# The delta rule's chain first in the scheduler, and the second block's convolutions straight from PSUM, in a two-block float32 kernel

## The chip, the cores and the metric

One NeuronCore of a Trainium2 chip runs the whole program. The metric is the time of one execution in microseconds (us), as the device measures it; a single profiled execution gives the trace from which all durations below are read. The engines carry the profile's names: PE is TensorE (matmuls, with its weight loads shown apart as PEld), DVE is VectorE, ACT is ScalarE, POOL is GpSimd, and SP is the engine whose queue issues most of the DMAs.

## The reference

A sequence of 256 tokens of width 1024 passes through two blocks in float32. The first has two layers of feed-forward network, hybrid mixer and feed-forward network. The second, where nearly all of the change lies, mixes tokens in two ways side by side and ends with a mixture of experts (MoE) with 32 experts. Its gated delta rule takes most of what follows:

```
def gated_deltanet(q_in, k_in, v_in, z, a, b, conv_w, a_log, dt_bias, out_norm):
    qkv = causal_conv_silu(jnp.concatenate([q_in, k_in, v_in], axis=-1), conv_w)
    q, k, v = jnp.split(qkv.astype(jnp.float32), 3, axis=-1)
    q = l2_norm(q...) * (HEAD_DIM ** -0.5);  k = l2_norm(k...)
    ...
    m = jnp.where(strict, jnp.einsum('bhncd,bhnsd->bhncs', kb, k) * decay, 0.0)
    t_mat = lax.linalg.triangular_solve(eye + m, eye, left_side=True, lower=True)
    ...
    o = rms_norm(o, out_norm) * jax.nn.silu(zf)

def sliding_window_attention(q, k, v, q_norm, k_norm, sinks, positions):
    q = rope(rms_norm(q, q_norm), positions);  k = rope(rms_norm(k, k_norm), positions)
    ...
```

`causal_conv_silu` is a convolution of four taps along the tokens with a SiLU behind it; `rope` turns pairs of elements by the cosine and sine of position times frequency.

## The kernel before

A float32 matmul is made of three products of rounded parts: weights and activations are each split into a high and a low part (fp32r), and high times high, low times high and high times low are summed in PSUM. ACT makes the high part (L304) and DVE the low part (L305).

In block 2 the input projection is done in pieces, in the order of `BLOCK2`: `q` and `k` (queries, keys and values of the attention), `n` (the gates), `2 3` (the two convolved column groups of the delta rule's keys), `0 1` (its queries), `4 5` (its values), `z` (its output gate). `S`, `G` and `V` start three generators beside them: the attention (`swa`), the delta rule (`gdn`) and its queries and values (`gqv`). A generator issues some instructions and yields; the planner goes round them. Instructions are then placed by a scheduler that fills each engine's queue, and code within `high_priority` goes ahead there by the number in `PRIO`. What a reader sees in a trace is each engine's queue, worked off strictly in its order.

The projection's column groups go through `fm`: for each half of 128 columns, `fm` multiplies the high weights with both activation parts at once (512 wide, L398), and the low weights with the high part (256 wide, L401). The two parts lie in one PSUM tile side by side and have to be added: ACT copies one to SBUF (L179) and DVE adds the other (L181). `conv2` then makes four taps of it, one on ACT (L1339) and three on DVE (L1341), and the SiLU (ACT L1344, DVE L1345). Three PSUM tiles (`pj`) hold the projection's sums, so that a new column group starts when the one three before it has been read. `z_out` reads z's sums on ACT (L1300) and DVE (L1301).

The chain of the delta rule is long. PE sums the squares of the keys (L1388); a reciprocal square root follows (`rsqrt_w`, L321 to L326, on DVE and ACT); sk (L1444) is broadcast by PE (L1453); four products with decays give gMT (L1480). The triangular solve is an explicit inverse: the 32 x 32 diagonal blocks are masked (L1593), transposed, and solved row by row in a loop of 15 steps on DVE (L1612, L1614), spread out as gX and gXt (L1619, L1622, L1625), and then joined to larger blocks by matmuls (from L1654 and L1673). In the attention, rotary angles and norms (L1712 to L1723) come ahead of transposes (L1745), scores (L1760 to L1762) and products (L1780, L1790). The end of the block is the output projection, 512 wide (L342 to L345), into which the two halves of the delta rule's output enter through gzo (L1537, L1541).

Of the kernel before, what the change touches and what calls it, by code (L numbers as in the profile page):

```python
# [7 lines left out]
F32 = mybir.dt.float32  # L8
# [3 lines left out]
AF = mybir.ActivationFunctionType  # L12
ALU = mybir.AluOpType
# [6 lines left out]
KD = 8  # L20
# [5 lines left out]
EPS2 = 1e-6  # L26
# [2 lines left out]
         'c1 x3 x4 x2 z2 z3 MB g0:0 g2:0 JS g2:3 g2:2 g2:1 g0:2 w2 g0:3 g1:0 JD g0:1 g1:2 w0 g1:3 g1:1 JM w1')  # L29
BLOCK2 = 'q n 2 3 S V G 0 k 4 1 z 5'  # L30

PRIO = {'narrow': 300, 'rope2': 300}

SPARE, SPARE2 = (1, 2), (1,)

# [71 lines left out]
class Net:  # L107
# [272 lines left out]

    def fm(self, xT, w, c0, fn):
        st = {}

        def tile(j):
            def run(wh, wl):
                xh, xl = xT()
                if j == 0:
                    st["a"] = (wh, wl)  # L390
                    return
                mm = self.nc.tensor.matmul
                for q in range(2):
                    ps = self.pj.tile([128, 512], F32, name="ps", tag="ps")
                    c = slice(q * 128, q * 128 + 128)
                    for k in range(KD):
                        h = (st["a"] if k < 4 else (wh, wl))[0]
                        mm(ps.rearrange("p (a b) -> p a b", a=2), h[:, k % 4, c], xh.both(k), start=k == 0, stop=False)  # L398
                    for k in range(KD):
                        l = (st["a"] if k < 4 else (wh, wl))[1]  # L400
                        mm(ps[:, 0:256], l[:, k % 4, c], xh[:, k, :], start=False, stop=k == KD - 1)  # L401
                    fn(q, ps[:, 0:256], ps[:, 256:512])
            return run

        for j in range(2):
            self.W(w[:, 4 * j:4 * j + 4, c0:c0 + 256], 4, 256, tile(j))
# [744 lines left out]
        nc.vector.tensor_scalar(v, v, -1.0, None, op0=ALU.mult)  # L1151


    def rope2(self, tabs):
        nc, I = self.nc, self.I
        P = self.sc([128, 2], I32, "pos")
        nc.sync.dma_start(P, I["positions_2"].rearrange("o (t p) -> p (o t)", p=128))
        for _ in range(5):
            yield
        pf = self.sc([128, 2], F32, "posf")  # L1160
        nc.vector.tensor_copy(pf, P)
        r = self.sc([128, 2, 2, 32], F32, "ang")
        c, s = r[:, 0, :, :], r[:, 1, :, :]
        for tb in range(NB):
            nc.vector.tensor_scalar(c[:, tb, :], self.inv2, pf[:, tb:tb + 1], None, op0=ALU.mult)
        n = self.sc([128, 2, 32], F32, "nrot")
        ts, stt = nc.vector.tensor_scalar, nc.vector.scalar_tensor_tensor
        for m in (4096.0, 1.0):
            ts(n, c, 1.0 / (TWO_PI * m), None, op0=ALU.mult)
            ts(n, n, ROUND, None, op0=ALU.add)  # L1170
            ts(n, n, -ROUND, None, op0=ALU.add)
            for q in PI_PARTS:
                stt(c, n, -q * m, c, op0=ALU.mult, op1=ALU.add)
        ts(c, c, 3.1415925, -3.1415925, op0=ALU.min, op1=ALU.max)
        nc.scalar.activation(s, c, AF.Sin)
        nc.scalar.activation(c, c, AF.Abs)
        ts(c, c, -1.0, math.pi / 2, op0=ALU.mult, op1=ALU.add)
        nc.scalar.activation(c, c, AF.Sin)
        self.rot = {}
        for g in ("q_norm_2", "k_norm_2"):  # L1180
            T = tabs[:, len(self.rot), :, :, :]
            gv = self.v2[g].rearrange("p (a b) -> p a b", a=2)
            for tb in range(NB):
                for i, x in enumerate((c, s)):
                    nc.vector.tensor_tensor(T[:, tb, i, :].rearrange("p (a b) -> p a b", a=2), gv,
                                            x[:, tb:tb + 1, :].to_broadcast([128, 2, 32]), op=ALU.mult)
            self.rot[g] = T


    def modulation(self, ss):  # L1190
# [72 lines left out]
    def block2(self, S_, us):  # L1263
        nc, I = self.nc, self.I
        w = I["w_in_2"][0].rearrange("(k p) n -> p k n", p=128)
        xT = lambda: S_["xT"]
        B = {"done": set(), "pj": False}
        self.B = B

        def alloc():  # L1270
            B["QVc"], B["KB"] = (self.t8([128, 8, S], F32, n) for n in ("gqv", "gkk"))
            t = self.big.tile([128, 2048], F32, name="sqkv", tag="b8")
            B["QV"] = t[:, 0:1536].rearrange("p (t n) -> p t n", t=2)
            self.active.append((self.rope2(t[:, 1536:2048].rearrange("p (g t i d) -> p g t i d", g=2, t=2, i=2)), 1, "rope2"))
            B["zO"] = self.t8([128, 4, 512], F32, "gzo")
        self.DO(alloc)


        def merged(i):
            if ("m", i) not in B:  # L1280
                t = self.t8([128, 8, S], F32R, "merged")
                B["m", i] = (t[:, 0:4, :], t[:, 4:8, :])
            return B["m", i]
        B["merged"] = merged

        def q_out(*ps):
            for tb in range(NB):
                nc.scalar.copy(B["QV"][:, tb, 0:512].rearrange("p (j a d) -> p a j d", a=2, j=4),
                               ps[tb].rearrange("p (a j d) -> p a j d", a=2, j=4))
            B["done"].add("q")  # L1290

        def kv_out(*ps):
            for tb in range(NB):
                nc.scalar.copy(B["QV"][:, tb, 512:768], ps[tb])
            B["done"].add("kv")

        def z_out(*ps):
            for tb in range(NB):
                z = B["zO"][:, tb, :]
                nc.scalar.activation(z, ps[tb], AF.Tanh, scale=0.5)  # L1300
                nc.vector.scalar_tensor_tensor(z, z, 1.0, ps[tb], op0=ALU.add, op1=ALU.mult)  # L1301
            B["done"].add("z")

        B["prefetch"] = lambda: us[0]["gu"]()
        first = True
        for it in BLOCK2.split():
            if it == "q":
                self.tok(xT, w, 2064, q_out, lead=first, spare=SPARE2)
            elif it == "n":
                self.narrow(xT, w, 2048, lambda pd: self.gates(B, pd))  # L1310
            elif it == "k":
                self.tok(xT, w, 2576, kv_out, n=256, lead=first)
            elif it == "z":
                self.tok(xT, w, 1536, z_out, lead=first)
            elif it == "G":
                self.GO(lambda: self.gdn(B), "gdn")
            elif it == "S":
                self.GO(lambda: self.swa(B), "swa")
            elif it == "V":
                self.GO(lambda: self.gdn_qv(B), "gqv")  # L1320
            else:
                j = int(it)
                self.fm(xT, w, j * 256, self.joined(lambda ps, j=j: self.conv2(B, j, ps)))
            first = False
        self.JOIN("swa")
        self.DO(lambda: (B.update(pj=True), B["head"]()))
        wo = I["w_out_2"][0].rearrange("(k p) n -> p k n", p=128)
        pre, fn, B["head"] = self.gated(S_, B)
        self.outp(lambda k: [a[:, k % 4, :] for a in B["m", k // 4]], wo, KD, fn, pre=pre, order=(4, 5, 6, 7, 0, 1, 2, 3),
                  join={4: "gdn"}, pre_at=4, tail=lambda: us[1]["gu"]())  # L1330
# [93 lines left out]
    def gdn(self, B):  # L1424
        nc = self.nc
        heads = lambda a: a.rearrange("p (h d) -> p h d", h=8)
        wide = lambda a, n=8: a.rearrange("p (h o) -> p h o", o=1).to_broadcast([128, n, 64])
# [7 lines left out]
        g, nG, eG = B["g"], B["nG"], B["eG"]  # L1435
        flat = lambda a: a.rearrange("p t h -> p (t h)")

        ps = self.squares(B, kT)
        rk = self.ln_p.tile([128, 3, 8], F32, name="rk", tag="rk")
        lk = self.ln_p.tile([128, 2, 8], F32, name="lk", tag="lk")  # L1440
        sk = self.ln_p.tile([128, 2, 8], F32, name="sk", tag="sk")
        self.rsqrt_w(flat(rk[:, 0:2, :]), flat(ps), 1.0, 4.0 * EPS2)
        yield
        nc.vector.tensor_tensor(sk, rk[:, 0:2, :], B["beta"], op=ALU.mult)  # L1444
        nc.vector.tensor_tensor(rk[:, 2, :], rk[:, 0, :], eG[:, 1, :], op=ALU.mult)
        nc.scalar.activation(lk, rk[:, 0:2, :], AF.Ln)
        nc.vector.tensor_tensor(nG, nG, lk, op=ALU.add)
        for tb in range(NB):
            t = slice(tb * 128, tb * 128 + 128)
            pb = bank([128, 4, 128])  # L1450
# [12 lines left out]
        MT = self.t8([128, 16, 128], F32, "gMT")  # L1463
# [115 lines left out]
    def inverse(self, B, MT, Xt):  # L1579
# [10 lines left out]
        A = self.sc([128, 512], F32, "sub")  # L1590
        for g in range(4):
            p = slice(32 * g, 32 * g + 32)
            tt(A[p, :].rearrange("p (i x m) -> p i x m", i=16, x=2), MT[p, :, p].rearrange("p m (x i) -> p i x m", x=2),  # L1593
               half[p, :].rearrange("p (o x u) -> p o x u", o=1, u=1).to_broadcast([32, 16, 2, 16]), op=ALU.mult)
        yield
        E = self.sc([128, 512], F32, "sub")
        nc.vector.transpose(E, A)
# [721 lines left out]
    def early(self, L):  # L2319
        for _ in range(6):  # L2320
            yield
        self.setup1()
        yield
        yield from self.setup2()
        yield from self.columns(0, L[0])

    def network(self, S_, out):
# [63 lines left out]
```

## Time and profile before

| | us |
|---|---|
| three runs | 2116.33, 2114.21, 2116.43 (median 2116.33) |
| the profiled execution | 2114.26 |
| span of its instructions | 2112.5 |
| mean granted clock of PE | 0.989 of full speed |

The profiled execution is 2.07 us under the median of the runs. Start times below count from the span's start; block 2's projection begins at about 1,640 us and its output projection ends at 1,818 us.

### The profile page before, as it was taken

The numbers are of one execution on the slowest core, as the hardware profiler recorded it, in microseconds if no ns is written. First come the engines' busy times: TensorE is split into PE (matmuls) and PEld (weight loads), VectorE is DVE, ScalarE is ACT, GpSimd is POOL, SyncE is SP. The second block draws the span as 40 slices with busy tenths as digits, with TensorE's granted clock in tenths as the row PEclk, the third lists the DMA queues.
The fourth block names the chain that finished last, engine by engine and source line by source line (L and its number), as shares of the span: only waits on it lengthen the run. The fifth ranks groups of instructions, "written<-read, shape, count | busy, mean of one in ns | idle before, by whom it ended". The sixth has DMA issues, their size and how long they took to land.

```text
span 2112.5 us, 30668 instructions
## 1 busy us (share of the span) xinstructions
PE 2053.8 (97%) x11411; PEld 1642.9 (78%) x11411; DVE 1477.7 (70%) x2785; ACT 1098.8 (52%) x2021; POOL 79.9 (4%) x65
## 2 busy tenths in 40 slices
PE   8999999999999999999999999999998989799998
PEld 7887877888888888888877888888887878545553
DVE  6876688987888667785688896877756885733332
ACT  6554565777655544553565776755543744211211
POOL 0000000100000000000000110000000200101000
PEclk9999999999999999999999999999999979999999
DMA  8875544454668676876544365575674323799895
GB/s 254 293 250 173 174 130 124 140 162 130 201 199 299 198 241 205 272 240 200 160 131 141 106 179 153 162 229 156 185 238 145 103 83 126 264 382 354 339 399 197
DMA packets 278825, 428.64 MB, mean 203 GB/s; under 512 B 21550, under 2 KB 206096, under 8 KB 277648
## 3 DMA queue, kind: packets, MB, share of 16 engines
q1 hardware_dynamic: 278240, 423.48, 61.7%
q0 software_dynamic: 432, 3.15, 0.4%
q8 instruction: 92, 1.51, 0.3%
q14 instruction: 61, 0.50, 0.1%
HBM read 425.50 MB, written 1.07 MB: 202 GB/s over the span
## 4 chain that ended last, share of the span: by engine, by line
PE 86%; DVE 9%; ACT 2%; issue 1%; POOL 1%; DMA 1%; SPq 0%; ACTq 0%; POOLq 0%; DVEq 0%
PE ps L398 27%; PE ps L401 14%; PE ps L2067 6%; PE y L342 5%; PE y L343 5%; PE y L345 4%; PE ps L2109 3%; PE ps L342 3%; PE ps L345 3%; PE ps L343 3%; DVE lo L305 2%; PE y L2122 2%; PE ps L2214 1%; PE y L331 1%; DVE cv L947 1%
## 5 line engine op out<-in xcount | busy, mean ns | idle before, releaser
L305 DVE TENSOR_TENSOR lo<-raw,hi 128x1024 fp32r<-128x1024 f32 (+1 forms) x556 | 659.0, 1194 | 250.1 <-ACT hi L304 172.7
L304 ACT CAST hi<-raw 128x1024 fp32r<-128x1024 f32 (+1 forms) x556 | 556.3, 1028 | 329.0 <-PE y L345 169.3
L398 PE MATMUL ps<-xhl,hi 128*128 128x512 f32 x2336 | 595.9, 396 | 5.2 <-DVE gzo L1301 4.4
L398 PEld LDWEIGHTS ps<-xhl,hi 128*128 128x128 f32 x2336 | 420.3, 189 | 84.0 <-DVE gzo L1301 4.6
L401 PEld LDWEIGHTS ps<-xhl,lo 128*128 128x128 f32 x2336 | 319.3, 190 | 23.0
L401 PE MATMUL ps<-xhl,lo 128*128 128x256 f32 x2336 | 328.6, 283 | 0.0
L342 PE MATMUL y<-hi,hh 128*128 128x512 f32 x352 | 137.3, 390 | 0.0
L343 PE MATMUL y<-lo,hh 128*128 128x512 f32 x352 | 137.0, 389 | 0.0
L342 PE MATMUL ps<-hi,xhl 128*128 128x512 f32 (+1 forms) x304 | 121.3, 401 | 5.7 <-DVE subt L1612 2.7
L2067 PE MATMUL ps<-wgu,hi 128*64 128x512 f32 x512 | 121.0, 594 | 0.0
L343 PE MATMUL ps<-lo,xhl 128*128 128x512 f32 (+1 forms) x304 | 120.0, 395 | 0.0
L345 PE MATMUL ps<-hi,xhl 128*128 128x512 f32 (+1 forms) x304 | 118.5, 392 | 1.2 <-DVE xhl L305 1.2
L179 ACT ACTIVATE ysum<-ps 128x256 f32<-128x256 f32 x180 | 68.8, 382 | 87.4 <-PE ps L401 83.2
L345 PE MATMUL y<-hi,hl 128*128 128x512 f32 x352 | 104.5, 389 | 0.0
L2067 PEld LDWEIGHTS ps<-wgu,hi 128*64 128x64 f32 x512 | 42.4, 137 | 69.1 <-issue 66.5
L181 DVE TENSOR_TENSOR ysum<-ysum,ps 128x256 f32<-128x256 f32 x180 | 74.2, 414 | 29.3 <-ACT ysum L179 28.8
L342 PEld LDWEIGHTS y<-hi,hh 128*128 128x128 f32 x352 | 66.1, 188 | 14.8 <-issue 0.8
L345 PEld LDWEIGHTS y<-hi,hl 128*128 128x128 f32 x352 | 66.1, 188 | 13.7
L343 PEld LDWEIGHTS y<-lo,hh 128*128 128x128 f32 x352 | 66.1, 188 | 13.5
L342 PEld LDWEIGHTS ps<-hi,xhl 128*128 128x128 f32 x304 | 58.0, 191 | 21.3 <-issue 4.4
L179 ACT ACTIVATE sg<-ps 128x256 f32<-128x256 f32 x80 | 30.5, 381 | 84.5 <-PE ps L401 84.4
L304 ACT CAST yh<-yg 128x512 fp32r<-128x512 f32 (+1 forms) x34 | 21.0, 618 | 99.3 <-DVE yg L2111 99.3
(610 smaller groups left out, 3075.0 us busy)
## 6 DMA issues: line engine op xcount, KB each, us to landing
raw<-in_w_mix_in_dram SPq DMA_DIRECT2D x184, 512.0 KB
raw<-in_ffn_w_in_dram SPq DMA_DIRECT2D x176, 512.0 KB
raw<-in_ffn_w_out_dram SPq DMA_DIRECT2D x88, 512.0 KB
wgu<-in_w_gate_dram SPq DMA_DIRECT2D x64, 512.0 KB
wgu<-in_w_up_dram SPq DMA_DIRECT2D x64, 512.0 KB
lo<-in_w_down_dram SPq DMA_DIRECT2D x54, 512.0 KB
wada<-in_w_ada_dram SPq DMA_DIRECT2D x96, 256.0 KB
raw<-in_w_branch_dram SPq DMA_DIRECT2D x48, 512.0 KB
```

Of the source, the lines that this page charges most:

```text
L179: self.nc.scalar.activation(out, pb, AF.Copy, scale=scale)
L181: self.nc.vector.tensor_tensor(out, out, pa, op=ALU.add)
L304: self.nc.scalar.copy(hi, src)
L305: self.nc.vector.tensor_tensor(lo, src, hi.bitcast(F32), op=ALU.subtract)
L342: mm(y, ah[:, t], wh[:, c], start=start, stop=False)
L343: mm(y, ah[:, t], wl[:, c], start=False, stop=False)
L345: mm(y, al[:, t], wh[:, c], start=False, stop=stop)
L398: mm(ps.rearrange("p (a b) -> p a b", a=2), h[:, k % 4, c], xh.both(k), start=k == 0, stop=False)
L401: mm(ps[:, 0:256], l[:, k % 4, c], xh[:, k, :], start=False, stop=k == KD - 1)
L2067: mm(gu[64 * e:64 * e + 64, c], u["x"](k)[:, 64 * e:64 * e + 64], w, start=k == 0 and i == 0, stop=k == KD - 1 and i == len(ws[0]) - 1)
L2109: mm(y[64 * e:64 * e + 64, :], u["hT"][:, k, 64 * e:64 * e + 64], wd[k][:, c], start=k == 0, stop=k == 1)
L2122: mm(ys[tb][n], u["PT"][p, tb, :], u["y"][n][i][p, :], start=start and i == 0, stop=stop and i == 1)
```

## The change

There are five edits. The generator `gdn` gets priority 500 in the scheduler. The convolutions of block 2 use three products 256 wide into one whole sum, so that `conv2` reads PSUM with no addition before it. The rotary angles move from `rope2` in block 2 to a generator in the first layer's feed-forward network, with the DMA of the positions; the eight multiplications with the norms' weights stay. The reciprocal square root of the keys' norms goes from five instructions on DVE and ACT to one on DVE and a power on POOL, and the logarithm is taken of the sum in place of the root. Half of the four masks at the head of the inverse go to ACT, as two activations each.

```
-PRIO = {'narrow': 300, 'rope2': 300}
+PRIO = {'narrow': 300, 'rope2': 300, 'gdn': 500}
...
+                if not wide:
+
+                    ps = self.pj.tile([128, 512], F32, name="ps", tag="ps").rearrange("p (a b) -> p a b", a=2)
+                    for q in range(2):
+                        c = slice(q * 128, q * 128 + 128)
+                        for k in range(KD):
+                            h, l = st["a"] if k < 4 else (wh, wl)
+                            self.mm3(ps[:, q, :], h[:, k % 4, c], l[:, k % 4, c], xh[:, k, :], xl[:, k, :], k == 0, k == KD - 1)
+                    fn(ps)
+                    return
...
-    def rope2(self, tabs):
+    def angles(self):
...
-        r = self.sc([128, 2, 2, 32], F32, "ang")
+        self.cs = r = self.const.tile([128, 2, 2, 32], F32, name="ang")
...
+    def rope2(self, tabs):
+        nc = self.nc
+        c, s = self.cs[:, 0, :, :], self.cs[:, 1, :, :]
...
-                self.fm(xT, w, j * 256, self.joined(lambda ps, j=j: self.conv2(B, j, ps)))
+                self.fm(xT, w, j * 256, lambda ps, j=j: self.conv2(B, j, ps), wide=False)
...
-        self.rsqrt_w(flat(rk[:, 0:2, :]), flat(ps), 1.0, 4.0 * EPS2)
+        nc.vector.tensor_scalar(flat(lk), flat(ps), 1.0, 4.0 * EPS2, op0=ALU.mult, op1=ALU.add)
+        nc.gpsimd.tensor_tensor(flat(rk[:, 0:2, :]), flat(lk), self.mhalf[:, 0:16], op=ALU.pow)
+        nc.scalar.activation(lk, lk, AF.Ln)
         yield
...
-        nc.scalar.activation(lk, rk[:, 0:2, :], AF.Ln)
-        nc.vector.tensor_tensor(nG, nG, lk, op=ALU.add)
+        nc.vector.scalar_tensor_tensor(nG, lk, -0.5, nG, op0=ALU.mult, op1=ALU.add)
...
+            if g % 2:
+                for x in range(2):
+                    nc.scalar.activation(av[:, :, x, :], mv[:, :, x, :], AF.Identity, scale=half[p, x:x + 1])
+            else:
+                tt(av, mv, half[p, :].rearrange("p (o x u) -> p o x u", o=1, u=1).to_broadcast([32, 16, 2, 16]), op=ALU.mult)
...
+        yield from self.angles()
         yield from self.columns(0, L[0])
```

The change moves instructions as well as replacing them; line numbers after the change are 16 to 21 higher here (L1614 becomes L1635, L1619 becomes L1640, L1625 becomes L1646, L1654 becomes L1675, L1301 becomes L1317, L1412 becomes L1428). The first place is DVE's queue at the end of the loop of 15 steps. Before, the loop's last reductions (L1614) are followed almost at once by the spreading (L1619, L1622, L1625), and z's two readings (L1301) stand behind it:

```order
L1614 TENSOR_REDUCE subz<-subt_17054 128x7
L1794 TENSOR_SCALAR sqkv<-y,smx 128x64
L1619 TENSOR_TENSOR sub<-subz,raw 128x512
L1794 TENSOR_SCALAR sqkv<-y,smx 128x64
L1622 STREAM_TRANSPOSE sub<-sub 128x512
L1619 TENSOR_TENSOR sub<-subz,raw 128x512
L1625 COPY gXt<-sub 32x16x2x16 x4
L1622 STREAM_TRANSPOSE sub<-sub 128x512
...
L1301 SCALAR_TENSOR_TENSOR gzo<-gzo,ps 128x512 x2
```

After the change the loop's last reduction (L1635) comes in one run with the steps before it, and a row of other work stands between it and the spreading (L1640):

```order
L1635 TENSOR_REDUCE subz<-subt_17100 128x7
...
L1317 SCALAR_TENSOR_TENSOR gzo<-gzo,ps 128x512
...
L1416 TENSOR_SCALAR eq<-y 128x16
L1317 SCALAR_TENSOR_TENSOR gzo<-gzo,ps 128x512
L1785 TENSOR_REDUCE smx<-y 128x1
L1786 TENSOR_REDUCE smx<-y 128x1
L1428 TENSOR_TENSOR gAT<-gAT,y 128x512
L1787 TENSOR_TENSOR smx<-smx,rq 128x2
L1428 TENSOR_TENSOR gAT<-gAT,y 128x512
L1788 TENSOR_SCALAR smx<-smx,vec_472 128x2
L1815 TENSOR_SCALAR sqkv<-y,smx 128x64 x2
L1640 TENSOR_TENSOR sub<-subz,raw 128x512
```

The spreading was moved behind both readings of z and behind eq, the sum of the queries' squares, with two products (L1428) that take eq's result on the way.

The second place is PE's queue at the first matmul of the inverse on gX. Before, one 512-wide matmul of the last convolved group (`5`) stands ahead of it, and the rest of that group, 7 of L398 and 8 of L401, behind it:

```order
L1411 MATMUL y<-gqv,gkk 128x128 x8
L401 MATMUL ps<-xhl,lo 128x256 x3
L398 MATMUL ps<-xhl,hi 128x512
L1654 MATMUL y<-gX,gC 128x128 x4
L1790 MATMUL y<-sqkv,wT 128x64
```

After, the whole group `5` (L299 to L301) and the router's small product (L1846, before L1825, which stood far behind) are ahead of it:

```order
L299 MATMUL ps<-xhl,hi 128x256
L300 MATMUL ps<-xhl,hi 128x256
L301 MATMUL ps<-xhl,lo 128x256
L1846 MATMUL ps<-hi,mod 128x36 x8
L1675 MATMUL y<-gX,gC 128x128 x4
L1811 MATMUL y<-sqkv,wT 128x64
```

The last half of a column group and the router's product were moved from behind the inverse's first matmul to ahead of it.

The third place is POOL's queue around the norms. Before, the first power of the attention's queries (rq, 8 columns) runs ahead of the clearing of gX (L1586), and that of gXt (L1587) comes last:

```order
L1718 TENSOR_TENSOR sq_16682<-sqkv 128x512
L314 TENSOR_TENSOR rq<-rq,mhalf 128x8
L314 TENSOR_TENSOR ss8b<-ss8b,mhalf 128x2
L1586 MEMSET gX 128x2048
L314 TENSOR_TENSOR ss8b<-ss8b,mhalf 128x2
L314 TENSOR_TENSOR rq<-rq,mhalf 128x8
L1718 TENSOR_TENSOR sq_16746<-sqkv 128x512
L1587 MEMSET gXt 128x2048
```

After, the new power of 16 columns (L1459) stands in the queue, and both clearings come ahead of the powers of rq:

```order
L314 TENSOR_TENSOR ss8b<-ss8b,mhalf 128x2
L1459 TENSOR_TENSOR rk<-lk,mhalf 128x16
L1739 TENSOR_TENSOR sq_16706<-sqkv 128x512
L1603 MEMSET gX 128x2048
L1604 MEMSET gXt 128x2048
L314 TENSOR_TENSOR rq<-rq,mhalf 128x8
L314 TENSOR_TENSOR ss8b<-ss8b,mhalf 128x2
L314 TENSOR_TENSOR rq<-rq,mhalf 128x8
L1739 TENSOR_TENSOR sq_16770<-sqkv 128x512
```

The clearings moved ahead of the attention's second set of norms, whose product on POOL (L1739, before L1718) now ends the row.

## Rows read from the trace of the kernel before

**Rows 1.** The page, part 1: busy time of each engine over the span

```profile
PE 2053.8 (97%) x11411; PEld 1642.9 (78%) x11411; DVE 1477.7 (70%) x2785; ACT 1098.8 (52%) x2021; POOL 79.9 (4%) x65
```

**Rows 2.** Windows: stretch, its length, busy of each engine, clock, DMA, GB/s

```profile
1695.60:1718.20 22.60, 19.95 (x95) 16.80 (x95) 19.61 (x72) 10.70 (x20) 0.61 (x1) 0.84 0.37 117
1718.20:1732.20 14.00, 8.48 (x42) 6.32 (x41) 13.09 (x29) 6.93 (x13) 2.00 (x3) 0.74 0.10 11
1732.20:1779.80 47.60, 46.35 (x352) 40.07 (x353) 27.13 (x75) 24.12 (x62) 7.55 (x6) 0.90 0.36 122
```

**Rows 3.** PE's waits, 1640 to 1850: line, releaser, us, times, longest

```profile
PE ps L398 <- DVE gzo L1301: 4.4, 1, 4.4
PE ps L1541 <- DVE gzo L1537: 3.1, 2, 1.7
PE ps L342 <- DVE subt L1612: 2.7, 1, 2.7
PE y L1654 <- ACT gX L1625: 1.2, 1, 1.2
PE y L1453 <- DVE sk L1444: 0.7, 1, 0.7
```

**Rows 4.** The chain of waits, 1640 to 1850: start, us, what

```profile
1721.19 0.96 DVE sub L1619
...
1732.21 2.05 PE y L1654 x8
...
1751.38 0.89 PE y L1654 x8
...
1759.39 1.71 PE ps L1825 x16
```

**Rows 5.** DVE in time, 1660 to 1733: start, us, instruction [idle before <- releaser]

```profile
1690.59 4.25 DVE L1593 TENSOR_TENSOR sub<-gMT,raw 32x512 f32<-32x512 f32 x4
...
1697.72 0.15 DVE L1612 TENSOR_TENSOR subt<-subz,subm 128x1 f32<-128x1 f32 x1
...
1713.03 0.17 DVE L1400 TENSOR_SCALAR eq<-y 128x16 f32<-128x16 f32 x1 [2.80 <-PE y L1388]
...
1720.58 0.43 DVE L1614 TENSOR_REDUCE subz<-subt 128x8 f32<-128x120 f32 x2
...
1729.51 1.28 DVE L1301 SCALAR_TENSOR_TENSOR gzo<-gzo,ps 128x512 f32<-128x512 f32 x2
```

**Rows 6.** DVE and POOL in time around the keys' norms

```profile
1667.40 0.17 DVE L321 TENSOR_SCALAR rsx<-y 128x16 f32<-128x16 f32 x1 [1.16 <-PE y L1388]
1674.18 0.16 DVE L1444 TENSOR_TENSOR sk<-rk,beta 128x16 f32<-128x16 f32 x1
1674.27 1.66 POOL L314 TENSOR_TENSOR rq<-rq,mhalf 128x8 f32<-128x8 f32 x1 [1.16 <-DVE ss8b L313]
1675.91 0.69 POOL L314 TENSOR_TENSOR ss8b<-ss8b,mhalf 128x2 f32<-128x2 f32 x1
1676.56 1.80 POOL L1586 MEMSET gX<- 128x2048 f32 x1
1681.77 2.75 POOL L314 TENSOR_TENSOR rq<-rq,mhalf 128x8 f32<-128x8 f32 x1
```

**Rows 7.** PE in time, group `4`: starts show the pace

```profile
1668.62 2.00 PE L398 MATMUL ps<-xhl,hi 128*128 128x512 f32 x8
1670.46 1.12 PE L401 MATMUL ps<-xhl,lo 128*128 128x256 f32 x8
1671.41 2.00 PE L398 MATMUL ps<-xhl,hi 128*128 128x512 f32 x8
```

**Rows 8.** Lines by form, block 2: min/median/max ns, first and last start

```profile
L181 DVE TENSOR_TENSOR ysum<-ysum,ps x12: 399/412/422, 1646.6 to 1755.9; 128x256 f32<-128x256 f32 x12
```

**Rows 9.** DVE's waits, 1732 to 1780

```profile
DVE gXt L1674 <- PE y L1673: 9.2, 7, 2.5
```

**Rows 10.** Windows: the first layer's feed-forward network

```profile
25.00:100.00 75.00, 75.00 (x430) 65.93 (x431) 61.35 (x99) 49.23 (x76) 0.00 (x0) 1.00 0.84 275
```

More of the change, by code (lines that the diff above doesn't have):

```diff
@@ L379, in tok, with fm @@
             self.W(w[:, kn * j:kn * j + kn, c0:c0 + n], kn, n, tile(j), lead and j in spare)
-    def fm(self, xT, w, c0, fn):
+    def fm(self, xT, w, c0, fn, wide=True):
         st = {}
@@ L1157, in rope2 @@
         nc.sync.dma_start(P, I["positions_2"].rearrange("o (t p) -> p (o t)", p=128))
-        for _ in range(5):
-            yield
+        yield
         pf = self.sc([128, 2], F32, "posf")
         nc.vector.tensor_copy(pf, P)
-        r = self.sc([128, 2, 2, 32], F32, "ang")
+        self.cs = r = self.const.tile([128, 2, 2, 32], F32, name="ang")
         c, s = r[:, 0, :, :], r[:, 1, :, :]
@@ L1178, in rope2 @@
         nc.scalar.activation(c, c, AF.Sin)
+        yield
+    def rope2(self, tabs):
+        nc = self.nc
+        c, s = self.cs[:, 0, :, :], self.cs[:, 1, :, :]
         self.rot = {}
@@ L1187, in rope2 @@
             self.rot[g] = T
+            yield
     def modulation(self, ss):
@@ L1592, in inverse @@
             p = slice(32 * g, 32 * g + 32)
-            tt(A[p, :].rearrange("p (i x m) -> p i x m", i=16, x=2), MT[p, :, p].rearrange("p m (x i) -> p i x m", x=2),
-               half[p, :].rearrange("p (o x u) -> p o x u", o=1, u=1).to_broadcast([32, 16, 2, 16]), op=ALU.mult)
+            av, mv = A[p, :].rearrange("p (i x m) -> p i x m", i=16, x=2), MT[p, :, p].rearrange("p m (x i) -> p i x m", x=2)
+            if g % 2:
[3 more added lines that the diff above has]
+                tt(av, mv, half[p, :].rearrange("p (o x u) -> p o x u", o=1, u=1).to_broadcast([32, 16, 2, 16]), op=ALU.mult)
         yield
```

## The prediction

> **What bounds the kernel now.** The page's first part comes first: PE is busy for 97% of the span [rows 1], so the time is PE's work plus PE's idle and slow time, and a change that only unloads another engine is worth what PE waits for it. The early stretch, where the angles are to go, shows PE busy for 75.00 of 75.00 us, with DVE at 61.35 and ACT at 49.23 [rows 10]: both have room.
>
> In block 2 the windows [rows 2] show where PE is short of work. From 1695.6 to 1732.2 us PE is busy for 19.95 + 8.48 = 28.4 of 36.6 us, at a mean clock of 0.84 and then 0.74, and there DVE is nearly full (19.61 of 22.6, then 13.09 of 14.0). From 1732.2 to 1779.8 us, the inverse and the attention, PE is busy for 46.35 of 47.6 us at a clock of 0.90 and DVE has time to spare (27.13); DVE waits there for PE, 9.2 us on L1673 alone [rows 9]. So DVE holds the first stretch and PE the second.
>
> PE's waits name the places [rows 3]: 2.7 us at z's third PSUM tile, 4.4 us at the last column group, which needs the tile that L1301 reads, 1.2 us at the first L1654, which needs gX, 0.7 us at sk, and 3.1 us in two pieces at gzo, under the output projection. In time [rows 5] the loop of 15 steps begins at 1697.72 and ends at 1720.58 + 0.43 = 1721.0 us, and DVE idles in it for 2.80 us, at eq, which waits for a product on PE. The spreading starts at 1721.19 and the first L1654 at 1732.21, 11.0 us later [rows 4].
>
> Part of the loss is the clock. The same eight L1654 take 2.05 us at 1732.21 and 0.89 us at 1751.38 [rows 4]: the first run at 1.2 GHz, the second at 2.4, and PE had idled for 4.4 us shortly before the first.
>
> **The change part by part.** I follow the start of the inverse's first matmul, and then what PE still has to do behind it.
>
> *Convolutions.* Eight L398 take 1670.46 - 1668.62 = 1.84 us and eight L401 1671.41 - 1670.46 = 0.95 us [rows 7]: 2.79 us for half a group. After, 24 products at L401's pace take 24 x 0.119 = 2.85 us. Twelve halves make 12 x 0.06 = +0.7 us of PE. DVE loses 12 x 0.41 = 4.9 us of additions [rows 8], and as many copies leave ACT. The taps read PSUM in their place; L181 reads PSUM too, 256 columns in 0.41 us, so I give the taps no surcharge. But the one tile is held until ACT's tap and three DVE taps of both halves are through, one after the other. In z this can cost PE a wait at its second or third tile: 0 to 2.7 us (the wait that is there now), I take 1.6.
>
> *Keys' norms.* From L321 at 1667.40 to L1444 at 1674.18 the chain takes 6.8 us [rows 6]. After, one DVE instruction (0.17), the power, and L1444 (0.16). No row shows a power of 16 columns: 2 columns take 0.69 and 8 take 1.66, so 0.16 a column, and an estimate for 16 is 1.66 + 8 x 0.16 = 2.9 us; the same 8 columns also took 2.75 [rows 6], so the other end is 4.0. The chain becomes 3.3 to 4.4 us. The keys' squares stand later in PE's queue, though, behind some 15 more products at 0.119 us: 1.8 us, so sk is ready at 1667.4 + 1.8 + 3.3 to 4.4 = 1672.5 to 1673.6, against 1674.18. PE comes there with 13 of the 48 matmuls of group `4` done instead of 26 of 32, so it waits longer, 2.2 us for 0.7 (bounds 0.7 and 3.6); the matmuls left over follow, so this is idle time, not work.
>
> The second value of the power has a rule beside it. The Trainium skill's page "SBUF — State Buffer", section "Who interferes with whom", says that a DVE instruction with two SBUF inputs and a GpSimd instruction that reads SBUF block each other for a whole instruction. By it the new power, next to L305 in DVE's queue, would take the longer time and sk would come at 1673.6; the rows of 1.66 and 2.75 for one form agree that something blocks it, and the sum would change by 1.1 us of a wait.
>
> *POOL's queue.* The power and both clearings (1.80 us each [rows 6]) now stand ahead of the attention's second rotation, which ends the row on POOL. That rotation's transposes on PE come right after group `4`, and PE would stand there for up to 3.5 us (two clearings at 1.80); lower end 0, if the clearings run while PE still has group `4`. I take 3.5.
>
> *Masks, angles.* The four masks take 4.25 us on DVE [rows 5]; two go to ACT, so the loop starts 2.1 us earlier by that, and 3 us with the rotary instructions gone: 1694.7 for 1697.72. In the loop, the additions, two L305 and the 2.80 us at eq go, so it takes 23.3 - 0.8 - 2.4 - 2.8 = 17.3 us and ends near 1712 for 1721. The angles' 22 small instructions cost nothing in the early stretch: DVE has 75 - 61.35 = 13.7 us there. If that cover is gone, the price is the one more table load of ACT's order, 1.3 us at most.
>
> *The spreading.* Here the gain is given back. In DVE's queue L1640 stands behind both L1317, eq, two L1428 and two L1815. L1317 waits for the end of z on PE, near 1711.8; eq waits for squares that ACT makes behind z's readings, near 1716; L1428 and L1815 wait for products of PE that use eq's neighbours. I put L1640 at 1721, where L1619 is now. An L305 stands between it and the copies (1.1 us), so the first matmul on gX starts at 1721 + 11.0 + 1.1 = 1733.1, which is 0.9 later than 1732.2. Bounds: 1726, six us earlier, if everything in that row is ready when the loop ends; 1738 if eq comes 5 us later.
>
> *Work behind it.* By then PE has done the whole of group `5` and the router's product. Before, 7 L398 and 8 L401 came behind (1.61 + 0.95 = 2.56 us [rows 7]) and L1825 (1.71 us [rows 4]): 4.3 us leave the stretch from 1732 to 1779. PE's time allows it: 28.4 us of the 36.6 were busy, and the waits above (2.2, 3.5, 1.6) are 7.3 us against 0.7 + 2.7 + 4.4 = 7.8 now. Since PE holds that stretch, I take all 4.3; the other end is 0, if the inverse's steps wait for DVE and ACT as soon as the filling is gone. Between the last gzo and the end of the block the projection has 18 matmuls for cover instead of 15: 3 x 0.23 = 0.7 us of the 3.1 us of waits.
>
> **Sum** against the profiled execution: +0.9 - 4.3 - 0.7 = -4.1 us; the +0.7 of the convolutions lies ahead of the first matmul on gX and is covered there by the wait for it. 2114.3 - 4.1 = 2110.2. That execution lies 2.1 us under the median of the runs, so against the median: 2112.2, say 2112.
>
> **The rivals.** *The chain comes early.* If L1640 is not held and follows the loop at 1715, the first matmul on gX starts at 1727: -5 - 4.3 - 0.7 = -10, 2106. For it: the loop does end some 9 us earlier. Against it: the queue's order.
>
> *Nothing is gained.* The stretch from 1732 keeps its 47.6 us because each step of the inverse waits for the copy before it, and L1640 stays: +0.9, 2117. For it: PE's slow clock there (0.90) would stay too, since PE idles ahead of the first L1675 as it does now. Against it: DVE waits for L1673, not the reverse.
>
> *eq is late (slower).* ACT makes the queries' squares behind z's readings and the attention's exponentials. DVE then stands at eq, and the inverse moves with it one for one. At 1720 this eats the gain, and from 1724 the kernel is slower by over 0.2%; at 1725 it is +9 - 4.3 = +5, 2121. For it: eq already held DVE for 2.80 us [rows 5]. Against it: z would have to end 8 us later than I think, or ACT's queue be as full as DVE's was.
>
> **How the numbers follow.** The forecast's case has 0.40, the early chain 0.20, no gain 0.20, and late eq 0.20. The range goes from 2105, just beyond the early chain, to 2121. A measurement of this kernel tells about 0.2% (4.2 us) from no change: below 2112.1 is faster. The early chain and half of the forecast's case lie there: 0.42. Late eq gives 0.20 slower, and 0.38 is left for the same.
>
> **What would show it.** Right: no wait for a PSUM tile at L1301's successor; DVE's loop ending near 1712 and L1640 not before 1719; the first L1675 near 1733; none of group `5` behind it; the stretch from there to the last inverse matmul near 43 us. Wrong: L1640 next to the loop's end (the early chain), an idle DVE at eq beyond 1720 (slower), a stretch of 47 us with PE waiting for gY or gXt (no gain), or PE waits of several us in the first 100 us, which would mean that the angles are not covered.

## The result

The changed kernel takes 2136.12 us (median of four runs, 2133.82 to 2138.37), the kernel before 2115.89 in the runs beside it: a ratio of 1.0096, with a 95% interval of 1.0084 to 1.0108. It is 20 us slower. I had forecast 2112, 4 us faster, with 2105 to 2121 as the range. The profiled execution after is the slowest of its four (2138.37) and the one before lies below its median, so their spans differ by 24.1 us, 4 more than the medians.

In the profile after, the page's first part (busy time of each engine over a span of 2136.6 us, before 2112.5) shows DVE and ACT a few us lighter, as meant, and PE 16 us busier than in [rows 1], although by my sum only 0.7 us of matmul work was added:

```profile
PE 2070.0 (97%) x11507; PEld 1663.1 (78%) x11507; DVE 1472.0 (69%) x2768; ACT 1092.7 (51%) x2008; POOL 81.4 (4%) x66
```

The waits of PE from 1640 to 1860 us (line, releaser, us in total, times, longest) answer to [rows 3]. The two that were to go are gone, at z's tile and at the last column group. Two that I had expected in their place are there, at sk (2.2) and at the second rotation (3.1); the wait for gX grew from 1.2 to 3.1. Behind the router's wait (`onehot`, its choice of experts), which was 8.5 us before, the largest is one that I had not expected: four waits for `pr`, the attention's exponentials (0.6 us before).

```profile
PE y L2008 <- DVE onehot L2005: 10.5, 1, 10.5
PE y L1801 <- ACT pr L1791: 6.4, 4, 1.6
PE y L1766 <- DVE sqkv L1744: 3.1, 1, 3.1
PE y L1675 <- ACT gX L1646: 3.1, 1, 3.1
PE y L1470 <- DVE sk L1462: 2.2, 1, 2.2
```

The windows after (stretch, length, busy of each engine, clock, DMA, GB/s), cut at the first matmul on gX and at the first of the output projection, show where the time went. The first stretch answers to the row from 1732.20 to 1779.80 in [rows 2]:

```profile
1736.60:1794.20 57.60, 50.20 (x321) 43.64 (x322) 23.08 (x70) 23.55 (x62) 7.54 (x6) 0.77 0.22 76
1794.20:1842.00 47.80, 46.26 (x247) 38.42 (x247) 18.07 (x30) 11.85 (x20) 3.83 (x3) 0.86 0.60 208
```

The stretch of the inverse and the attention takes 57.6 us for 47.6, and that of the output projection 47.8 us. Before, the second ran as follows, at full clock:

```profile
1779.80:1818.30 38.50, 35.42 (x226) 29.40 (x223) 17.26 (x30) 10.71 (x18) 3.84 (x3) 1.00 0.64 229
```

So of 24.1 us between the two spans, 4.4 come from a later first matmul on gX (1736.63 for 1732.21), 10.0 from the first stretch and 9.3 from the second; I had put +0.9, -4.3 and -0.7 there. The first stretch has more idle time (7.4 us for 1.3) and a lower clock (0.77 for 0.90), though 31 matmuls fewer. The second has less idle time (1.5 us for 3.1) but a lower clock, and some of the router's matmuls more.

### The profile page after: what moved, and what is told of

It reads as the page before. It is cut to its first block, busy times and chain, and to the rows that moved or that the text cites. A ratio compares the mean times of both kernels' runs of the same rounds, so it can differ in the third digit from the quotient of the medians.

```text
span 2136.6 us, 30846 instructions
## 1 busy us (share of the span) xinstructions
PE 2070.0 (97%) x11507; PEld 1663.1 (78%) x11507; DVE 1472.0 (69%) x2768; ACT 1092.7 (51%) x2008; POOL 81.4 (4%) x66
## 4 chain that ended last, share of the span: by engine, by line
PE 87%; DVE 8%; ACT 2%; issue 2%; POOL 1%; DMA 0%; SPq 0%; POOLq 0%; ACTq 0%; DVEq 0%
PE ps L408 27%; PE ps L411 14%; PE ps L2088 6%; PE y L342 5%; PE y L343 5%; PE y L345 4%; PE ps L2130 3%; PE ps L342 3%; PE ps L345 3%; PE ps L343 3%; DVE lo L305 2%; PE y L2143 2%; PE ps L2235 1%; PE y L331 1%; PE ps L301 1%
## 5 line engine op out<-in xcount | busy, mean ns | idle before, releaser
L305 DVE TENSOR_TENSOR lo<-raw,hi 128x1024 fp32r<-128x1024 f32 (+1 forms) x556 | 659.6, 1195 | 246.6 <-ACT hi L304 174.6
L408 PE MATMUL ps<-xhl,hi 128*128 128x512 f32 x2240 | 568.5, 395 | 0.8 <-DVE kc L181 0.8
L408 PEld LDWEIGHTS ps<-xhl,hi 128*128 128x128 f32 x2240 | 402.7, 189 | 75.7 <-issue 3.3
L411 PEld LDWEIGHTS ps<-xhl,lo 128*128 128x128 f32 x2240 | 306.2, 191 | 21.6
L411 PE MATMUL ps<-xhl,lo 128*128 128x256 f32 x2240 | 314.8, 283 | 0.0
L179 ACT ACTIVATE ysum<-ps 128x256 f32<-128x256 f32 x168 | 64.1, 382 | 75.9 <-PE ps L411 75.7
L181 DVE TENSOR_TENSOR ysum<-ysum,ps 128x256 f32<-128x256 f32 x168 | 69.5, 416 | 27.8 <-ACT ysum L179 27.6
L342 PEld LDWEIGHTS ps<-hi,xhl 128*128 128x128 f32 x304 | 57.7, 190 | 18.9 <-ACT qs L795 3.0
L345 PEld LDWEIGHTS ps<-hi,xhl 128*128 128x128 f32 x304 | 57.6, 190 | 15.5 <-DVE xhl L305 4.3
```

The lines of the kernel that those rows point to most:

```text
L179: self.nc.scalar.activation(out, pb, AF.Copy, scale=scale)
L181: self.nc.vector.tensor_tensor(out, out, pa, op=ALU.add)
L305: self.nc.vector.tensor_tensor(lo, src, hi.bitcast(F32), op=ALU.subtract)
L342: mm(y, ah[:, t], wh[:, c], start=start, stop=False)
L345: mm(y, al[:, t], wh[:, c], start=False, stop=stop)
```

## The experiments

**First: which edit?** Four kernels take the priority or the convolutions alone, or leave one of them out. Two theories stand against each other: the first, that PE lost the work that filled its idle time beside the inverse, the second, that the priority itself makes the attention's steps late. What decides between them is the order behind the first matmul on gX: in the changed kernel nothing of the last column group is left there.

The priority alone:

```
-PRIO = {'narrow': 300, 'rope2': 300}
+PRIO = {'narrow': 300, 'rope2': 300, 'gdn': 500}
```

> The kernel before with the priority of gdn alone; all else as before. In this order 17 matmuls of the last column group and the router's product still stand behind the inverse's first matmul on gX, and 54 matmuls of the output projection behind the last gzo instead of 30. Theory 1 (the work that filled PE beside the inverse and the attention was moved ahead of it, and without it PE idles at each attention step and its clock falls): the filling is there, so about the time of before, 2112 to 2120. Theory 2 (with its priority gdn takes DVE's and ACT's queues ahead of the attention, whose steps then come late for PE, whatever fills PE): most of the 20 us are here, 2130 to 2140.

It took 2127.44 us, a ratio of 1.0054 (1.0037 to 1.0071): between the ranges of the two theories and in neither.

All edits but the priority:

```
-PRIO = {'narrow': 300, 'rope2': 300, 'gdn': 500}
+PRIO = {'narrow': 300, 'rope2': 300}
```

> The changed kernel without the priority of gdn; all four other edits stay. 16 matmuls of the last group and the router's product stand behind the first matmul on gX. Theory 1: the filling is back, so 2108 to 2118. Theory 2: without the priority the loss is gone, also 2108 to 2118. Both theories fall if it stays above 2128: then the loss is one of the other edits by itself.

It took 2114.06 us, 0.9993 (0.9983 to 1.0003), as both theories had it.

The new convolutions alone:

```
-                self.fm(xT, w, j * 256, self.joined(lambda ps, j=j: self.conv2(B, j, ps)))
+                self.fm(xT, w, j * 256, lambda ps, j=j: self.conv2(B, j, ps), wide=False)
```

> The kernel before with the convolutions from whole sums alone, without the priority. By its order none of the last column group and none of the router's product is left behind the first matmul on gX, as in the changed kernel, but the queues have no priority for gdn and the output projection keeps its 30 matmuls behind the last gzo. Theory 1: the stretch beside the inverse has no filling, so it loses as the changed kernel does there, 2126 to 2138. Theory 2: no priority, no loss, 2110 to 2120.

It took 2104.26 us, 0.9942 (0.9926 to 0.9959), the fastest kernel of the study and 6 us below the second theory's range.

All edits but the convolutions, which is the changed kernel with that line undone:

> The changed kernel with the convolutions of before (two parts added on ACT and DVE). Nothing is left to fill behind the first matmul on gX, and the priority is there. Both theories: slow, 2128 to 2142; if it is near 2116, the convolutions from whole sums themselves cause the loss, by their longer hold on PSUM and not by the order.

It took 2131.29 us, 1.0077 (1.006 to 1.0094), slow as expected.

Theory 1 falls: the kernel with the new convolutions alone has no filling left in that stretch and is 11.6 us faster, and the kernel with the priority alone has its filling and is slower by as much. The loss goes with the priority: without it, all other edits together change nothing, and with it each kernel is slow. The two stretches in the windows of the kernel with the priority alone, of that with the convolutions alone, and of that with all edits but the priority:

```profile
1727.30:1782.60 55.30, 50.17 (x356) 43.91 (x355) 27.46 (x76) 24.22 (x64) 7.58 (x6) 0.86 0.33 108
1782.60:1832.00 49.40, 47.85 (x247) 39.80 (x247) 18.06 (x30) 11.85 (x20) 3.83 (x3) 0.83 0.57 199
```

```profile
1728.80:1771.90 43.10, 41.57 (x322) 36.33 (x322) 24.48 (x72) 23.36 (x61) 7.82 (x6) 0.88 0.35 123
1771.90:1810.40 38.50, 35.43 (x225) 29.42 (x223) 17.28 (x30) 10.71 (x18) 3.83 (x3) 1.00 0.63 227
```

```profile
1737.20:1779.90 42.70, 42.23 (x354) 37.43 (x354) 25.93 (x73) 23.25 (x61) 7.53 (x6) 0.96 0.40 136
1779.90:1818.40 38.50, 35.42 (x224) 29.42 (x223) 17.28 (x30) 10.71 (x18) 3.83 (x3) 1.00 0.63 228
```

Alone, the priority does bring the chain forward, to 1727.3 us, and then loses 7.7 us against [rows 2] in the first stretch and 10.9 in the second.

**Why the priority costs.** PE's timeline shows it (start, us, instruction, and in brackets the idle time before it with its releaser). First one round of the attention in the kernel with all edits but the priority: scores (L1782, L1783), then the inverse's products (L1713, L1675, L1694), the step's outputs (L1811 to L1813), and the transposes of `pr` (L1801), which wait for nothing:

```profile
1753.24 0.48 PE L1782 MATMUL y<-sqkT 64*128 64x128 f32 x2
1753.56 0.59 PE L1783 MATMUL y<-sqkT 64*128 64x256 f32 x2
1754.09 0.66 PE L1713 MATMUL y<-ctab,gXt 128*128 128x128 f32 x4
1754.58 1.06 PE L1675 MATMUL y<-gX,gC 128*128 128x128 f32 x8
1755.47 1.06 PE L1694 MATMUL y<-gXt,gY 128*128 128x128 f32 x8
1756.37 0.33 PE L1811 MATMUL y<-sqkv,wT 128*128 128x64 f32 x2
...
1756.98 0.28 PE L1801 MATMUL y<-ctab,pr 128*128 128x128 f32 x1
```

In the changed kernel the inverse's products come ahead of the scores, and between scores and transposes stand only the short outputs:

```profile
1755.26 1.06 PE L1675 MATMUL y<-gX,gC 128*128 128x128 f32 x8
1756.16 1.06 PE L1694 MATMUL y<-gXt,gY 128*128 128x128 f32 x8
1757.05 0.38 PE L1801 MATMUL y<-ctab,pr 128*128 128x128 f32 x2
1757.36 0.49 PE L1782 MATMUL y<-sqkT 64*128 64x128 f32 x2
1757.69 0.59 PE L1783 MATMUL y<-sqkT 64*128 64x256 f32 x2
1758.21 0.44 PE L1811 MATMUL y<-sqkv,wT 128*128 128x64 f32 x2
...
1760.70 0.47 PE L1801 MATMUL y<-ctab,pr 128*128 128x128 f32 x1 [1.60 <-ACT pr L1791]
```

From the scores' end (1757.69 + 0.59) to the transposes it takes 2.4 us for the softmax (maximum on DVE, exponentials on ACT). The inverse's products covered 2.3 us of that (1754.09 to 1756.37); now 1.6 lie bare in such a round.

The second theory had another reason: late steps on DVE and ACT, whose queues have the priority too. The traces speak against it. From the scores' end to the end of the first exponentials it takes 1756.60 - 1754.15 = 2.45 us in the round without the priority and 1760.55 - 1758.28 = 2.27 in the round with it:

```profile
1756.16 0.44 ACT L1791 ACTIVATE pr<-y,smx,rq 128x128 f32<-128x128 f32 x1
...
1760.11 0.44 ACT L1791 ACTIVATE pr<-y,smx,rq 128x128 f32<-128x128 f32 x1
```

The four rounds that lie bare take 2.2 to 2.3 us, five without the priority 2.1 to 4.6. The softmax is no slower with the priority; what is gone is PE's work beside it.

In the projection's stretch the wide matmuls moved as well. Behind the first four of them the changed kernel has a row of small ones with hardly a wide one between, and from about 1801 us it runs at the lower clock. PE's windows there (stretch, length, busy, clock, DMA, GB/s):

```profile
1794.20:1801.20 7.00, 7.00 (x49) 0.99 0.14 56
1801.20:1815.20 14.00, 14.00 (x56) 0.52 0.84 289
1815.20:1842.00 26.80, 25.26 (x145) 1.00 0.59 205
```

In the slow part twelve L1541 take 2.82 us, and 512-wide matmuls start 0.43 us apart:

```profile
1804.82 2.82 PE L1541 MATMUL ps<-v,gAT 128*128 128x64 f32 x12
...
1811.46 0.63 PE L342 MATMUL y<-hi,merged 128*128 128x512 f32 x1
1811.89 0.63 PE L343 MATMUL y<-lo,merged 128*128 128x512 f32 x1
```

With all edits but the priority sixteen L1541 take 2.00 us, 64 columns each, with nine wide matmuls shortly ahead of them and twelve behind, 0.23 us apart:

```profile
1791.32 2.00 PE L1541 MATMUL ps<-v,gAT 128*128 128x64 f32 x16
1793.12 0.48 PE L342 MATMUL y<-hi,merged 128*128 128x512 f32 x1
1793.44 0.39 PE L343 MATMUL y<-lo,merged 128*128 128x512 f32 x1
```

The next four kernels test this reading, which the texts below call theory 3. The first keeps all five edits and ends the priority where gX and gXt are spread; the second is its mirror image, the kernel with the convolutions alone and the priority from the spreading on (the test reads `not in`):

```
-                    if c[2] in PRIO:
+                    if c[2] in PRIO and not (c[2] == "gdn" and "spread" in self.B["done"]):
...
+        B["done"].add("spread")
         js = [slice(4 * q, 4 * q + 4) for q in range(4)]
```

> The changed kernel with all five edits, but gdn has its priority only until gX and gXt are spread. In its order the attention's scores stand ahead of the inverse's products again and the projection's wide matmuls between the small ones. Theory 3 (the priority's loss comes from the order of PE's queue behind the spreading: the softmax lies bare between scores and transposes, and the small matmuls stand in one row without wide ones, at the lower clock): the stretch from the first gX to the first matmul of the output projection falls from 57.6 to about 43 us, that of the projection from 47.9 to 38.5, in all about 2112 (2108 to 2116). Rival (the loss comes from the waits ahead of the spreading, at sk, at the second rotation and at eq, and the low clock that they leave): 2128 or more.

It took 2117.35 us, 1.0006 (0.9996 to 1.0015), 1.4 above theory 3's range and 11 below the rival's. Its stretches are 43.0 us and 38.5, as theory 3 had them:

```profile
1739.90:1782.90 43.00, 41.59 (x322) 36.16 (x322) 25.40 (x71) 23.22 (x61) 7.72 (x6) 0.89 0.32 111
1782.90:1821.40 38.50, 35.43 (x224) 29.42 (x223) 17.28 (x30) 10.70 (x18) 3.83 (x3) 1.00 0.65 230
```

> The kernel with the new convolutions alone (2104), with the priority of gdn only from the spreading on. Theory 3: all of the loss is here, 2104 + 10 to 15 in the stretch beside the attention + 9 to 11 in the output projection = 2122 to 2130. Rival: no loss, 2102 to 2110.

It took 2130.88 us, 1.0069 (1.005 to 1.0088), 26.6 more than the convolutions alone and just above the range. Its stretches are long again:

```profile
1732.10:1788.30 56.20, 47.89 (x324) 41.72 (x323) 23.45 (x70) 22.06 (x56) 6.29 (x5) 0.82 0.22 78
1788.30:1837.60 49.30, 47.76 (x247) 39.60 (x247) 18.07 (x30) 11.82 (x20) 3.83 (x3) 0.83 0.59 199
```

Against the convolutions alone they take 13.1 and 10.8 us more, and the first matmul on gX comes 3.3 us later. The priority behind the spreading is the cause of the loss. That PE's order is the way it works is read from the traces: no kernel changes that order alone.

The third asks what of the loss is the clock. It puts dummy matmuls, whose results nothing reads, into the waits:

```
             pt = bank([128, 3, 128])
+            for i in range(6):
+                nc.tensor.matmul(pt.rearrange("p a b -> p (a b)"), self.identb, m_win, start=True, stop=True)
             for i in range(3):
                 nc.tensor.transpose(pt[:, i, :], pr[:, i * 128:(i + 1) * 128], self.ident)
```

> The changed kernel with six dummy matmuls of 384 columns in bf16 ahead of the transposes of each of the eight attention steps (48 in all, about 0.16 us each at full clock, 8 us of work); they write into the tile that the transposes then overwrite, and nothing depends on them. If the idle waits for the softmax bring the lower clock, filling them raises the clock in that stretch and the total is not longer, 2126 to 2136, although PE has 8 us more to do; if the clock there has another cause, the work beyond the 6.4 us of waits adds, 2137 to 2142.

It took 2134.62 us, 1.0094 (1.0077 to 1.0111), within the first range: against the changed kernel the total tells no difference. But the stretch that was filled fell from 57.6 to 51.1 us although 36 of the 48 dummies and the router's sixteen products stand in it, and its clock rose from 0.77 to 0.97; the projection's stretch, where nothing was filled, was at 0.83 (0.86 in the changed kernel):

```profile
1735.60:1786.70 51.10, 48.41 (x374) 39.44 (x374) 23.75 (x70) 23.88 (x62) 7.58 (x6) 0.97 0.25 86
1786.70:1836.10 49.40, 47.86 (x247) 39.67 (x247) 18.08 (x30) 11.86 (x20) 3.83 (x3) 0.83 0.58 202
```

Part of the order also moved with the dummies (the router's products), and this profile is of the fastest of its four executions where that of the changed kernel is of the slowest. So this is a hint and no clean proof that the waits bring the clock down in the first stretch. It does show that the low clock of the projection's stretch is not brought along from the stretch ahead, which ran at 0.97.

The fourth adds the priority up to the spreading to the convolutions alone:

> The new convolutions with the priority of gdn only until the spreading; without the moved angles, the keys' norms and the masks. If the priority brings the chain's start forward here as it did alone (from 1732.2 to 1727.3) and theory 3 holds, 2098 to 2105; if the new convolutions already had all of that, 2102 to 2108.

It took 2107.49 us, 0.9956 (0.9939 to 0.9972): not faster than the convolutions alone, as the second range had it. Ahead of the spreading the priority gains nothing beside the convolutions: the two kernels that have it only there took 3.2 and 3.3 us more than the same kernels without it, which the intervals do not tell from nothing.

**Second: where the rest of the gain goes.** The convolutions alone are 10 us faster than all edits without the priority. Four kernels add the other edits to them, with the lines of the diff above.

> The new convolutions (2104 by themselves) and the keys' norms by a power on POOL; nothing else. The kernel with all edits but the priority took 2114, so one of the other three edits, or their meeting, costs 10 us. If it is the norms (the power of 16 columns and the clearings of gX and gXt in POOL's queue ahead of the second rotation): 2110 to 2116. If not: 2102 to 2107.

2107.84 us, 0.9964 (0.9952 to 0.9977): 1 us above the range without a loss, and not the 10 us.

> The new convolutions and the rotary angles moved to the start; nothing else. If the angles' move costs (attention's steps come earlier and in DVE's way): 2108 to 2116. If it is neutral or gains: 2100 to 2106.

2109.66 us, 0.9973 (0.9963 to 0.9983), in the range of a loss.

> The new convolutions and half of the masks on ACT; nothing else. The masks' 2.1 us on DVE are in the chain: a gain would be 2101 to 2104. If the four activations stand behind other work in ACT's queue and the transpose waits for them: 2106 to 2114.

2106.93 us, 0.9955 (0.9938 to 0.9972), in the range without a gain.

> The new convolutions, the angles and the masks, without the priority and without the norms on POOL. If the norms cost the 10 us by themselves: 2100 to 2106. If it is the sum of small losses of each: 2108 to 2112.

2107.38 us, 0.9968 (0.9955 to 0.998): between the two ranges.

None of the three is a gain on top of the convolutions, and each lies 2.7 to 5.4 us above them, which the intervals can't tell from nothing except for the angles alone (0.9963 to 0.9983 against 0.9926 to 0.9959). There is no single edit that costs the 10 us, and how they add up was not settled. The profiles show where it lies: the first matmul on gX starts at 1728.8 us with the convolutions alone and at 1737.2 with all three edits beside them, and the two stretches behind it are as long (43.1 and 38.5, 42.7 and 38.5). With the norms it starts at 1731.3, with the angles at 1734.0, with the masks at 1729.2, with angles and masks at 1730.0. The waits at sk point the same way: 1.1 us with the convolutions alone, 2.2 with all three edits.

## Why the prediction was wrong, step by step

**What bounds the kernel.** Right as a reading of the kernel before: the waits for z's tile and for the last group were there to be had. The convolutions alone took them away and were 11.6 us faster. In the profiles, 3.4 us of it is the earlier first matmul on gX (1728.8 for 1732.2) and 4.5 the shorter stretch behind it.

**Convolutions.** The 1.6 us that I charged at z's tile did not appear as a wait. A tap that reads PSUM takes what it took from SBUF (median 477 ns after, 476 before), so no surcharge was right.

**Keys' norms and POOL's queue.** The power of 16 columns took 2.90 us (estimate 2.9), the wait at sk 2.2 (2.2), and that for the second rotation 3.1 (3.5). That the wait at sk came out to the tenth is in part luck: sk was ready at 1675.08, behind my 1672.5 to 1673.6, and PE came there later too. POOL in time, where both clearings run ahead of the powers of rq:

```profile
1672.14 2.90 POOL L1459 TENSOR_TENSOR rk<-lk,mhalf 128x16 f32<-128x16 f32 x1 [2.67 <-DVE lk L1458]
1681.56 1.28 POOL L1739 TENSOR_TENSOR sq<-sqkv 128x512 f32<-128x512 f32 x1 [6.52 <-DVE ss8b L1733]
1682.77 1.82 POOL L1603 MEMSET gX<- 128x2048 f32 x1
```

The power was not blocked here, so the longer time by the Trainium skill's page "SBUF — State Buffer", section "Who interferes with whom", is not seen for it. The kernel with convolutions and norms agrees with that rule: its power of 2 columns that began inside an L305 (1668.44, 1.23 us) took 1.71 us, and the other one in that trace 0.69.

**Masks, angles.** The loop of 15 steps took 16.1 us (17.3), but it began at 1698.56 for my 1694.7, later than before the change. A square on POOL (L1739, before L1718), for which DVE waits shortly ahead of the masks and which now comes behind both clearings, ended 6.1 us later. I had priced POOL's queue for PE alone and put nothing for DVE. DVE's wait before and after:

```profile
1685.78 0.69 DVE L1719 TENSOR_TENSOR sqkv<-sqkv 128x512 f32<-128x512 f32 x1 [1.96 <-POOL sq L1718]
...
1691.88 0.69 DVE L1740 TENSOR_TENSOR sqkv<-sqkv 128x512 f32<-128x512 f32 x1 [2.57 <-POOL sq L1739]
```

From this row to the loop it took 11.9 us before (to 1697.72) and 6.7 after.

The angles were covered in the early stretch: PE's waits in the first 100 us are those of before, within 0.3 us.

**The spreading.** Right in kind, 3.5 us too early: the loop ended at 1714.7 us (forecast 1712), eq came at 1720.87 (1716), and L1640 at 1724.39 (1721), as these rows of DVE's timeline after show; the first matmul on gX started at 1736.63 (1733.1).

```profile
1720.87 0.17 DVE L1416 TENSOR_SCALAR eq<-y 128x16 f32<-128x16 f32 x1 [1.58 <-PE y L1404]
1724.39 1.78 DVE L1640 TENSOR_TENSOR sub<-subz,raw 128x512 f32<-128x512 f32 x1
```

**Work behind it: the step that failed.** I wrote that PE holds the stretch beside the attention, took 4.3 us of work out of it and expected 43 us. With the priority it takes 57.6: the term of -4.3 came out as +10.0. I had read in the order what moved ahead of the first matmul on gX, and had taken the order behind it as given. But a priority holds for the whole generator: it put the inverse's products ahead of the attention's scores in each round, and so took the cover from the softmax (6.4 us of waits, with the clock at 0.77). That PE hardly waits there was a property of that order and not of the stretch. Against the kernel with the priority up to the spreading (43.0 us, the same matmuls) 14.6 us were lost: 6.0 of idle time, and by the mean clocks some 8.5 more (0.23 of 57.6 less 0.11 of 43.0, an estimate).

The kernels without the priority behind the spreading do show 42.7, 43.1 and 43.0 us, but this does not make the sum right. The two of 43 have the work taken out, at a clock of 0.88 and 0.89; the one of 42.7 still has it (354 matmuls for 352 before) and is as short, at 0.96. So a like time came about in two ways, and a clock higher by 0.07 to 0.08 did there what the missing work did.

**Cover in the projection.** The sign was wrong: -0.7 became +9.3. I counted 18 wide matmuls for 15 (the traces show 18 and 14) between the last two steps as 0.7 us of gain, and the waits for gzo did fall, from 3.1 to 1.5 us. What I had not weighed is where the other wide matmuls went: 54 stand behind the last gzo, for 30 before, and so are missing from the row of small ones ahead of it. Of the 9.3 us some 2.3 are the router's transposes and products, which moved into that stretch; the 14.0 us at the lower clock cost about 7 (an estimate: half of it).

**The rivals.** None was this one. The slower rival put its price on eq, and its sign appeared: eq came 5 us later than I thought, with DVE idle for 1.58 us. That is part of the 4.4 us ahead of the first matmul on gX, not of the 19 behind it. The kernel with the priority up to the spreading alone, whose first matmul on gX is later still (1739.9), is not slower.

## What to carry to other kernels

A priority for one generator has to be checked at the far end of that generator as well as at the place it is meant for: in each round, ask what stood between the other generator's matmul and the instruction that waits for its softmax. Watch, too, where a change of order gathers the small matmuls: in this kernel the stretch with the wide ones between them ran at full clock in seven profiles of nine, and with the wide ones gathered at its end at 0.83 to 0.86 in all five. And where several edits come together, time them one by one: here one of five was worth 11.6 us, and another cost as much or, beside the rest, 22.

## What the runs showed of the hardware

In the projection's stretch the lower clock did not go with idle time. In the changed kernel PE idled for 1.5 us there, at a mean clock of 0.86; before the change for 3.1 us, at 1.00. The clock fell at about 1801 us to the lower level (1.2 GHz: 0.52 of full speed from 1801.2 to 1815.2) after some 6 us without a wait, in which PE ran matmuls of 64 columns and one of 512. It rose again (to 2.4 GHz) after a run of 512-wide ones. PE's order in this stretch is one of two in all fourteen profiles. The five kernels with the priority behind the spreading share the order of the changed kernel, at 0.83 to 0.86. The nine others share that of the kernel before, and seven of them run it at 1.00. So the clock goes with the order, but the order alone does not decide it: with the convolutions and the masks, in the very order of the kernel before, the clock fell as well, again without a wait of PE and in a row of small matmuls, though behind wide ones, and the stretch took 41.5 us for 38.5. PE's window there:

```profile
1776.80:1783.40 6.60, 6.60 (x27) 0.50 0.60 164
```

What else decides was not found.

In the stretch ahead of it, dummy matmuls of 384 columns went with a clock of 0.97 for 0.77 and a stretch of 51.1 us for 57.6, although they are work; with the reservations above.
